# Sums of the hidden activations formed in the first feed-forward product, and one ring of buffers for results and pairs

## The chip, the core and the metric

The kernel runs on one core of one Trainium2 chip. The metric is device time in microseconds for one execution. Its engines are named here as in the profile: PE is TensorE (PEld its weight loads), ACT ScalarE, DVE VectorE, POOL GpSimd, SP SyncE. Each takes its instructions in the order of its own queue.

## The reference, cut to what matters

One decoder layer over 512 positions of width 2048. After a mixing half (attention, gating, convolution), the feed-forward half is

```python
h = rms_norm(x, mlp_norm[l])
x = x + jnp.square(jax.nn.relu(h @ w_mlp_in[l])) @ w_mlp_out[l]
```

with `w_mlp_in` 2048 x 8192 and `w_mlp_out` 8192 x 2048, all float32. The change touches these two products alone.

## The kernel before, in words

**Three matmuls for a product.** Each float32 operand is split into a high part (a rounding copy on ACT, `high` or `split`) and a low part (a subtraction on DVE, `low` or `split`); high x high, high x low and low x high are added in PSUM (`mm3`, lines 161 to 163). Activations are held transposed, 128 features by 512 positions a tile; `xh` and `xl` hold 16 such tiles.

**Groups.** `stream` runs a list of groups. A plain group (`tr_group`) makes 4 (or 2) output tiles over 16 steps k, loading 512 KB of weights for every two k ("a piece"); after each k, `step()` runs one task from a queue. A `Strassen` group ("a block", two output tiles) makes its 256 x 512 result with seven products instead of eight, in an order of two-by-two block sums: weights are added and subtracted on DVE (`s1`, `s2`, `q`), and the activations' sums lie ready in `tt`. A "double" product uses one 512-column matmul for high x both parts and one of 256 columns (lines 867, 868), and one DVE add more to join the halves; a "triple" uses three of 256 columns.

**The two feed-forward products.** The first: a plain group of 4 tiles, 29 blocks (products 0, 1 and 3 double), a plain group of 2 tiles. Each result gets its scale, the relu and the square (`hidden`: DVE, then ACT) and is stored to `hd` in DRAM by POOL. The second runs in four chunks of 2048 hidden features: chunk 0 has a plain group, 4 blocks and a closing plain group; chunks 1 to 3 have 6 blocks and a closing group. Results of chunks 0 to 2 are added to `x1d` in DRAM by storing DMAs that accumulate (`finish_out`, line 1018, and `close_mlp_out`, which first copies PSUM to tile `co` on ACT, line 1042); chunk 3 adds `x1d` on DVE and writes the output.

**Preparing a chunk.** While a closing group of chunks 0 to 2 runs, tasks (`both_tasks`) load the next chunk's hidden tiles in pairs (tile `hr`), write `xh`, `xl`, and form the sums from the pair in place (`sums`, four subtractions of 256 columns, line 936 on) for `tt`. For chunk 0 `parts_tasks` does this in two passes over the pairs, during the last group of the first product and the first of the second.

**Buffers.** Ring `hp` has three places of two tiles (4 KB a partition) for the pairs. The results `c` of a block and `co` of a closing group share one place, tag `c`.

**Order.** `ordr` pins an instruction behind the one traced before it on its engine, where `ordered[0]` is true: from `open_last_in`, so in the whole second product. Before that (`evac_qk` sets it false) the compiler's scheduler orders instructions; loads on POOL are never pinned. In `stream`, the load of an item (with its casts and subtractions) is traced two items ahead (`AHEAD`), so casts of weights stand in ACT's queue ahead of, or behind, tasks and result copies.

Of the kernel before, what the change touches and what calls it, by code (L numbers as in the profile page):

```python
# [9 lines left out]
F32 = mybir.dt.float32  # L10
F32R = mybir.dt.float32r
AF = mybir.ActivationFunctionType
ALU = mybir.AluOpType
AX = mybir.AxisListType

P = 128
T = 512
TB = T // P
D = 2048
KT = D // P  # L20
DFF = 4 * D
# [5 lines left out]
KC = CHUNK_FF // P  # L27
# [13 lines left out]
def trunk_kernel(  # L41
# [12 lines left out]
    nc = tc.nc  # L54
# [5 lines left out]
    w1 = w1[0].rearrange("(k p) n -> p k n", p=P)  # L60
    w2 = w2[0].rearrange("(k p) n -> p k n", p=P)

    dram = ctx.enter_context(tc.tile_pool(name="dram", bufs=1, space=bass.MemoryType.DRAM))
# [19 lines left out]
    def uid():  # L83
        cnt[0] += 1
        return cnt[0]
# [5 lines left out]
    def ordr(ins):  # L91
        return tc.keep_in_program_order(ins) if ordered[0] else ins
# [7 lines left out]
    def flush():  # L100
        while tasks:
            step()
# [24 lines left out]
    xh, xl = xhl[:, 0], xhl[:, 1]  # L127
# [4 lines left out]
    rbc = cpool.tile([P, T], F32, name="rbc")  # L132
# [595 lines left out]
    mlp = {}  # L728
# [8 lines left out]

    x1d = [dram.tile([P, T], F32, name=f"x1d{n}") for n in range(KT)]
    hd = [dram.tile([P, T], F32, name=f"hd{n}") for n in range(DFF // P)]
    nch = DFF // CHUNK_FF  # L740

    def open_out(ng):
# [38 lines left out]
    TH = T // 2  # L781

    def sub(out, a, b):
        ordr(nc.vector.tensor_tensor(out=out, in0=a, in1=b, op=ALU.subtract))  # L784

    def add(out, a, b):
        ordr(nc.vector.tensor_tensor(out=out, in0=a, in1=b, op=ALU.add))
# [23 lines left out]
    def x1mov(k):  # L811
        return x1v[:, k, :, 0], x1v[:, k, :, 1]

    class Strassen:


# [37 lines left out]
        def product(self, j, h, l):  # L854
            sp, i = mlp["spool"], self.i
            if j == 0 and self.begin is not None:
                self.begin(self)
            if j == 2:
                flush()
            if j < 6:  # L860
                self.pv = main_ps(f"pt{j}{i}").rearrange("p (h t) -> p h t", h=2)
            pv, half, double = self.pv, int(j == 6), j in self.double
            for m in range(KT // 2):
                start, stop = m == 0, m == KT // 2 - 1
                bh, bl, both = self.factor(FACTOR[j], m)
                if double:
                    nc.tensor.matmul(pv, lhsT=h[:, m], rhs=both, start=start, stop=False)  # L867
                    last[0] = nc.tensor.matmul(pv[:, 1], lhsT=l[:, m], rhs=bh, start=False, stop=stop)  # L868
                else:
                    mm3(pv[:, half], (h[:, m], l[:, m]), (bh, bl), start, stop)  # L870

            def take(out, more):
                add(out, pv[:, half], more)
                if double:
                    add(out, pv[:, 1], out)

            if j == 0:

                self.c = sp.tile([P, 6, TH], F32, tag="c", name=f"c{i}")
                self.p = [sp.tile([P, TH], F32, tag=f"p{n}", name=f"p{n}{i}") for n in range(2)]  # L880
            c = self.c
            if j in (0, 3):
                p = self.p[j // 3]
                ordr(nc.scalar.copy(out=p, in_=pv[:, 0]))
                if double:
                    add(p, pv[:, 1], p)
            elif j == 1:
                take(c[:, 2], self.p[0])
            elif j == 2:
                take(c[:, 0], self.p[0])  # L890
            elif j == 4:
                take(c[:, 1], c[:, 0])
                add(c[:, 0:6:5], self.p[1].unsqueeze(1).broadcast_to([P, 2, TH]), c[:, 0:2])
            elif j == 6:
                add(c[:, 3:5], pv, c[:, 0:2])
                self.finish(self, c[:, 2:6].rearrange("p (f h) t -> p f (h t)", f=2))

    def open_quarters():
        flush()
# [3 lines left out]
    def hidden(c, src, rb):  # L903

        ordr(nc.vector.scalar_tensor_tensor(out=c, in0=src, scalar=0.0, in1=rb, op0=ALU.max, op1=ALU.mult))
        ordr(nc.scalar.activation(out=c, in_=c, func=AF.Square))

    def finish_in(g, c):
        hidden(c, c, rbc.unsqueeze(1).broadcast_to([P, 2, T]))
        for n in range(2):  # L910
            nc.gpsimd.dma_start(out=hd[g.c0 // P + n], in_=c[:, n])

    def c_tiles(pss, name):
        for j, ps in enumerate(pss):
            if j % 2 == 0:
                cc = mlp["spool"].tile([P, 6, TH], F32, tag="c", name=f"{name}{j}").rearrange("p (f h) t -> p f (h t)", h=2)
            yield j, ps, cc[:, j % 2]

    def close_mlp_in(pss, f0):
        for j, ps, c in c_tiles(pss, f"cn{f0}"):  # L920
            hidden(c, ps, rbc)
            nc.gpsimd.dma_start(out=hd[f0 + j], in_=c)


    def pair(name):
        return mlp["spool"].tile([P, 2, T], F32, tag="hp", name=f"{name}{uid()}", bufs=3)

    def load_pair(c, m):
        t = pair("hr")
        for n in range(2):  # L930
            nc.gpsimd.dma_start(out=t[:, n], in_=hd[c * KC + 2 * m + n])
        return t

    def sums(t):
        q = t.rearrange("p k (h t) -> p (k h) t", h=2)
        sub(q[:, 0], q[:, 1], q[:, 0])
        sub(q[:, 1], q[:, 3], q[:, 1])
        sub(q[:, 3], q[:, 3], q[:, 0])
        sub(q[:, 2], q[:, 2], q[:, 3])
        return q  # L940

    def high(dst, src):
        ordr(nc.scalar.copy(out=dst, in_=src))  # L943

    def low(dst, src, h):
        sub(dst, src, h.bitcast(F32))

    def parts_tasks(c):

        room = [load_pair(c, m) for m in range(3)]  # L950
        s = [slice(2 * m, 2 * m + 2) for m in range(8)]

        def parts(m):
            if m < 8:
                high(xh[:, s[m]], room[m])
            if m:
                low(xl[:, s[m - 1]], room[m - 1], xh[:, s[m - 1]])
                room.append(load_pair(c, (m + 2) % 8) if m < 9 else None)

        def rest(m):  # L960
            t = room[8 + m]
            q = sums(t)
            high(mlp["tt"][:, :, m, 0], q)
            return q

        kept = {}

        def even(m):
            kept[m] = rest(m)

        def odd(m):
            low(mlp["tt"][:, :, m, 1], kept[m], mlp["tt"][:, :, m, 0])
            if m + 3 < 8:
                room.append(load_pair(c, m + 3))

        out = [lambda m=m: parts(m) for m in range(9)]
        for m in range(8):
            out.extend([lambda m=m: even(m), lambda m=m: odd(m)])
        return out

    def both_tasks(c):

        room = {m: load_pair(c, m) for m in range(3)}
        kept = {}

        def tile_high(k):
            if k < KC:
                high(xh[:, k], room[k // 2][:, k % 2])

        def tile_low(k):  # L990
            if 0 <= k < KC:
                low(xl[:, k], room[k // 2][:, k % 2], xh[:, k])

        def even(m):
            tile_high(2 * m)
            tile_low(2 * m - 1)
            if m:
                kept[m - 1] = sums(room[m - 1])
                high(mlp["tt"][:, :, m - 1, 0], kept[m - 1])

        def odd(m):
            tile_high(2 * m + 1)
            tile_low(2 * m)
            if m:
                low(mlp["tt"][:, :, m - 1, 1], kept[m - 1], mlp["tt"][:, :, m - 1, 0])
                if m + 2 < KC // 2:
                    room[m + 2] = load_pair(c, m + 2)

        return [f for m in range(KC // 2 + 1) for f in (lambda m=m: even(m), lambda m=m: odd(m))]

    def open_last_in():
        ordered[0] = True
# [26 lines left out]

    def close_mlp_out(pss, c, f0):  # L1040
        for j, ps, t in c_tiles(pss, f"co{c}{f0}"):
            ordr(nc.scalar.copy(out=t, in_=ps))
            nc.gpsimd.dma_start(out=x1d[f0 + j], in_=t, accum_op=ALU.add)

    def close_last(pss, f0, j, ts):
        dst = mlp["acc"][j // 2][:, j % 2, ts]
# [3 lines left out]
    def hmov(k):  # L1050
        return xh[:, k], xl[:, k]

    groups = [
        qk_group(0, 0, x_chunk), qk_group(1, 0), qk_group(0, 1), qk_group(1, 1),
        nat_group(w_in[:, :, OFF_V:OFF_V + 256], 256, xstat, close_v1),
        nat_group(w_in[:, :, OFF_V + 256:OFF_V + 768], 512, xstat4, close_v23),
        nat_group(w_in[:, :, OFF_VA:OFF_VA + 512], 512, xstat, close_va),
        nat_group(w_in[:, :, OFF_U:OFF_U + 512], 512, xstat, close_u),
    ]
# [7 lines left out]
        ))  # L1067
    groups.append(tr_group(w1[:, :, :T], 4, x1mov, lambda pss: close_mlp_in(pss, 0)))
    for c0 in range(T, DFF - 2 * P, 2 * P):
        groups.append(Strassen(w1, c0, x1_factor, (0, 1, 3), finish_in))  # L1070
    groups.append(tr_group(
        w1[:, :, DFF - 2 * P:], 2, x1mov, lambda pss: close_mlp_in(pss, DFF // P - 2), before=open_last_in,
    ))
# [62 lines left out]
```

## Time and profile before

| | |
|---|---|
| median of 3 runs | 2100.81 us (2098.47 to 2101.3) |
| the profiled execution's own time | 2099.07 us |
| its span, first to last instruction | 2097.4 us |
| mean granted clock of TensorE | 0.987 |
| busy, share of the span | PE 97%, PEld 88%, DVE 67%, ACT 39%, POOL 8% |
| first feed-forward product | from about 740 to 1360 us |
| second | from there to the end |

A row of a timeline gives the start, the duration, the engine, the line, what is written and read, and in brackets how long the engine was idle before and what ended it. A duration spans an instruction's whole way through its engine; consecutive matmuls overlap, so their pace is read from start to start. A row of windows gives the busy time of each engine in a stretch, with the instructions' count; PEclk is the granted clock as a share of full speed, and the DMA share is the mean busy share of the 16 DMA engines.

### The profile page before, as it was taken

Reading aid. Unit: us, or ns where it says so; the run is one execution under the profiler, and the core shown is the slowest. Engines: PE = TensorE matmul, PEld = TensorE weight load, DVE = VectorE, ACT = ScalarE, POOL = GpSimd, SP = SyncE. Lnnn points to the kernel's source line nnn. Section 1 sums busy time; section 2 is a strip of 40 time slices with the busy share of each in tenths; the row PEclk is TensorE's granted clock in tenths of the full one; section 3 lists DMA queues with packets and bytes.
Section 4 is the critical chain, followed back from the end, with each engine's and each line's share of the span. In section 5 each row is a group of like instructions: output and inputs, shape, how many; then the busy total and the mean of one; then the engine's idle time right before and its main releaser. Section 6 shows DMA issues by size and latency. Waiting matters only on the chain.

```text
span 2097.4 us, 30649 instructions
## 1 busy us (share of the span) xinstructions
PE 2034.8 (97%) x12434; PEld 1836.2 (88%) x12434; DVE 1395.6 (67%) x1846; ACT 820.6 (39%) x1086; POOL 158.0 (8%) x270
## 2 busy tenths in 40 slices
PE   9999999999999999999999999998979997997999
PEld 9999888888888889999999999877869986986998
DVE  5443453534345588888888888577678776777882
ACT  5334442322234434444444444443343443343441
POOL 0000000100000010000000000121010011001110
PEclk9999999999999999999999999999989998998999
DMA  7323222433533355444444444566545555554542
GB/s 250 124 76 105 79 67 70 129 99 97 185 129 126 116 152 155 127 130 138 125 140 128 130 144 122 159 194 136 156 129 142 121 171 125 133 154 121 161 142 90
DMA packets 322045, 276.78 MB, mean 132 GB/s; under 512 B 12772, under 2 KB 271076, under 8 KB 321904
## 3 DMA queue, kind: packets, MB, share of 16 engines
q1 hardware_dynamic: 295744, 202.93, 33.0%
q0 software_dynamic: 23712, 67.67, 11.7%
q10 hardware_dynamic: 2448, 4.23, 0.6%
q8 instruction: 97, 1.59, 0.3%
q14 instruction: 44, 0.36, 0.1%
HBM read 237.01 MB, written 37.77 MB: 131 GB/s over the span
## 4 chain that ended last, share of the span: by engine, by line
PE 77%; DMA 8%; DVE 8%; ACT 4%; issue 2%; POOL 0%; SPq 0%; ACTq 0%; DVEq 0%
PE pt L161 16%; PE pt L163 16%; PE pt L162 16%; PE pt L867 10%; PE pn L161 5%; PE pt L868 5%; PE pn L162 5%; PE pn L163 5%; DMA x1d<-c 4%; DVE wl L262 3%; DVE hr L784 2%; DMA wq<-in_w_mlp_out_dram 2%; ACT wh L261 2%; DMA x1d<-co 1%; ACT tt L943 1%
## 5 line engine op out<-in xcount | busy, mean ns | idle before, releaser
L163 PE MATMUL pt<-xhl,wl 128*128 128x256 f32 (+1 forms) x1480 | 493.5, 333 | 3.3 <-DVE wl L262 3.3
L161 PE MATMUL pt<-xhl,wh 128*128 128x256 f32 (+1 forms) x1480 | 493.7, 334 | 1.5 <-ACT xhl L943 1.5
L162 PE MATMUL pt<-xhl,wh 128*128 128x256 f32 (+1 forms) x1480 | 493.4, 333 | 1.1 <-DVE xhl L784 1.1
L262 DVE TENSOR_TENSOR wl<-wr,wh 128x1024 fp32r<-128x1024 f32 (+2 forms) x199 | 213.8, 1074 | 343.9 <-ACT wh L261 287.9
L261 ACT CAST wh<-wq 128x1024 fp32r<-128x1024 f32 x255 | 267.7, 1050 | 378.5 <-PE pt L162 190.7
L262 DVE TENSOR_TENSOR wl<-wq,wh 128x1024 fp32r<-128x1024 f32 x255 | 311.3, 1221 | 82.0 <-ACT wh L261 81.1
L261 ACT CAST wh<-wr 128x1024 fp32r<-128x1024 f32 (+2 forms) x199 | 185.0, 930 | 399.0 <-PE pt L162 265.0
L163 PEld LDWEIGHTS pt<-xhl,wl 128*128 128x128 f32 x1480 | 281.7, 190 | 31.7 <-DVE wl L262 4.5
L162 PEld LDWEIGHTS pt<-xhl,wh 128*128 128x128 f32 x1480 | 281.7, 190 | 28.9 <-DVE xhl L784 1.8
L161 PEld LDWEIGHTS pt<-xhl,wh 128*128 128x128 f32 x1480 | 281.3, 190 | 29.3 <-ACT xhl L943 2.1
L163 PE MATMUL pt<-tt,wl 128*128 128x256 f32 x1048 | 297.6, 284 | 3.8 <-DVE wl L262 3.6
L161 PE MATMUL pt<-tt,wh 128*128 128x256 f32 x1048 | 296.9, 283 | 1.8 <-ACT wh L261 1.8
L162 PE MATMUL pt<-tt,wh 128*128 128x256 f32 x1048 | 296.7, 283 | 0.0
L867 PE MATMUL pt<-tt,wh 128*128 128x512 f32 x584 | 215.1, 408 | 42.4 <-ACT wh L261 42.4
L161 PEld LDWEIGHTS pt<-tt,wh 128*128 128x128 f32 x1048 | 199.8, 191 | 6.4 <-ACT wh L261 3.0
L163 PEld LDWEIGHTS pt<-tt,wl 128*128 128x128 f32 x1048 | 199.9, 191 | 5.8 <-DVE wl L262 5.5
L162 PEld LDWEIGHTS pt<-tt,wh 128*128 128x128 f32 x1048 | 199.9, 191 | 0.0
L161 PE MATMUL pn<-wh,xhl 128*128 128x384 f32 (+2 forms) x512 | 185.2, 364 | 1.4 <-DVE qn L440 1.3
L162 PE MATMUL pn<-wl,xhl 128*128 128x384 f32 (+2 forms) x512 | 179.5, 351 | 0.7 <-DVE wl L148 0.7
L163 PE MATMUL pn<-wh,xhl 128*128 128x384 f32 (+2 forms) x512 | 179.2, 350 | 0.0
L867 PEld LDWEIGHTS pt<-tt,wh 128*128 128x128 f32 x584 | 112.7, 194 | 68.3 <-ACT wh L261 44.0
L868 PE MATMUL pt<-tt,wl 128*128 128x256 f32 x584 | 166.8, 287 | 1.9 <-DVE wl L262 1.9
(208 smaller groups left out, 2992.0 us busy)
## 6 DMA issues: line engine op xcount, KB each, us to landing
wq<-in_w_mlp_in_dram SPq DMA_DIRECT2D x116, 512.0 KB, 4.1
wq<-in_w_mlp_out_dram SPq DMA_DIRECT2D x88, 512.0 KB, 5.4
hr<-hd POOLq DMA_DIRECT2D x80, 256.0 KB, 3.1
wr<-in_w_mlp_out_dram SPq DMA_DIRECT2D x40, 512.0 KB, 4.5
wr<-in_w_in_dram SPq DMA_DIRECT2D x144, 128.0 KB, 2.3
wr<-in_w_out_dram SPq DMA_DIRECT2D x32, 512.0 KB, 3.6
hd<-c POOLq DMA_DIRECT2D x58, 256.0 KB, 2.6
wr<-in_w_in_dram SPq DMA_DIRECT2D x24, 512.0 KB, 3.5
```

The lines of the kernel that those rows point to most:

```text
L161: nc.tensor.matmul(ps, lhsT=ah, rhs=bh, start=start, stop=False)
L162: nc.tensor.matmul(ps, lhsT=ah, rhs=bl, start=False, stop=False)
L163: last[0] = nc.tensor.matmul(ps, lhsT=al, rhs=bh, start=False, stop=stop)
L261: ordr(nc.scalar.copy(out=dst_h, in_=src))
L262: ordr(nc.vector.tensor_tensor(out=dst_l, in0=src, in1=dst_h.bitcast(F32), op=ALU.subtract))
L784: ordr(nc.vector.tensor_tensor(out=out, in0=a, in1=b, op=ALU.subtract))
L867: nc.tensor.matmul(pv, lhsT=h[:, m], rhs=both, start=start, stop=False)
L868: last[0] = nc.tensor.matmul(pv[:, 1], lhsT=l[:, m], rhs=bh, start=False, stop=stop)
L943: ordr(nc.scalar.copy(out=dst, in_=src))
```

## The change

Results `c`, `co` and the pairs share one ring `hp`, now of four places. In the first product each pair of hidden tiles is also turned into its four sums, in another place of that ring, and stored to a new DRAM tensor `hs` by one DMA of 512 KB. The second product loads these sums where it formed them: `both_tasks` has eight steps of two tasks, each step with a pair and its sums, two steps loaded ahead; `parts_tasks` loads the sums in its second pass. In the first product, product 0 alone stays double. The three result columns of `c` that were spare are gone, its indices move. The last group of the first product, and the sums of the last pair, take places of the weights' ring `wq`.

```diff
+    hs = [dram.tile([P, 4, T // 2], F32, name=f"hs{n}") for n in range(DFF // P // 2)]
...
+    def pair(name):
+        return mlp["spool"].tile([P, 2, T], F32, tag="hp", name=f"{name}{uid()}", bufs=4)
...
-                self.c = sp.tile([P, 6, TH], F32, tag="c", name=f"c{i}")
+                self.c = pair("c").rearrange("p f (h t) -> p (f h) t", h=2)
...
-                add(c[:, 0:6:5], self.p[1].unsqueeze(1).broadcast_to([P, 2, TH]), c[:, 0:2])
+                take(c[:, 2], c[:, 1])
+                add(c[:, 1:4:2], self.p[1].unsqueeze(1).broadcast_to([P, 2, TH]), c[:, 1:3])
...
+    def store_hidden(f, c):
+        for n in range(2):
+            nc.gpsimd.dma_start(out=hd[f + n], in_=c[:, n])
+        t = pair("ts") if f + 2 < DFF // P else quarter_room("ts")
+        q, o = (v.rearrange("p k (h t) -> p (k h) t", h=2) for v in (c, t))
+        sub(o[:, 0:2], q[:, 1:4:2], q[:, 0:2])
+        sub(o[:, 3], q[:, 3], o[:, 0])
+        sub(o[:, 2], q[:, 2], o[:, 3])
+        nc.gpsimd.dma_start(out=hs[f // 2], in_=o)
+
     def finish_in(g, c):
         hidden(c, c, rbc.unsqueeze(1).broadcast_to([P, 2, T]))
-        for n in range(2):
-            nc.gpsimd.dma_start(out=hd[g.c0 // P + n], in_=c[:, n])
-
-    def c_tiles(pss, name):
+        store_hidden(g.c0 // P, c)
+
+    def c_tiles(pss, name, room=None):
+        room = room or pair
         for j, ps in enumerate(pss):
             if j % 2 == 0:
-                cc = mlp["spool"].tile([P, 6, TH], F32, tag="c", name=f"{name}{j}").rearrange("p (f h) t -> p f (h t)", h=2)
-            yield j, ps, cc[:, j % 2]
+                cc = room(f"{name}{j}")
+            yield j, ps, cc
...
-    def sums(t):
...
+    def load_sums(c, m):
+        t = pair("hsr").rearrange("p k (h t) -> p (k h) t", h=2)
+        nc.gpsimd.dma_start(out=t, in_=hs[c * KC // 2 + m])
+        return t
...
+        def sums(m):
+            if m < 8:
+                high(mlp["tt"][:, :, m, 0], room[8 + m])
+            if m:
+                low(mlp["tt"][:, :, m - 1, 1], room[7 + m], mlp["tt"][:, :, m - 1, 0])
+                if m + 3 < 8:
+                    room.append(load_sums(c, m + 3))
+
+        return [lambda m=m: parts(m) for m in range(9)] + [lambda m=m: sums(m) for m in range(9)]
+
+    def both_tasks(c):
+
+        room = {}
+
+        def load(m):
+            room[m] = load_pair(c, m), load_sums(c, m)
 
         def even(m):
-            kept[m] = rest(m)
+            high(xh[:, 2 * m], room[m][0][:, 0])
+            high(mlp["tt"][:, :, m, 0], room[m][1])
 
         def odd(m):
...
+            high(xh[:, 2 * m + 1], room[m][0][:, 1])
+            low(mlp["tt"][:, :, m, 1], room[m][1], mlp["tt"][:, :, m, 0])
+            s = slice(2 * m, 2 * m + 2)
+            low(xl[:, s], room[m][0], xh[:, s])
+            if m + 2 < KC // 2:
+                load(m + 2)
+
+        load(0)
+        load(1)
+        return [f for m in range(KC // 2) for f in (lambda m=m: even(m), lambda m=m: odd(m))]
...
-        groups.append(Strassen(w1, c0, x1_factor, (0, 1, 3), finish_in))
+        groups.append(Strassen(w1, c0, x1_factor, (0,), finish_in))
```

## Rows read from the trace of the kernel before

**Rows 1.** Windows of 100 us; the sum is over all four such stretches.
```profile
core 0: us, PE busy (x) PEld busy (x) DVE busy (x) ACT busy (x) POOL busy (x), PEclk, DMA share, GB/s
1700.00:1800.00 100.00, 85.79 (x526) 76.32 (x525) 74.92 (x100) 40.91 (x52) 14.67 (x22) 0.93 0.52 132
...
sum 400.00, PE 345.31 PEld 311.82 DVE 300.55 ACT 159.24 POOL 59.11; mean PE 86.33 PEld 77.96 DVE 75.14 ACT 39.81 POOL 14.78
```

**Rows 2.** Waits, whole span: engine, line, waited for: us, times, longest.
```profile
DVE c L787 <- DMA x1d<-c: 50.1, 13, 4.6
...
PE pt L867 <- ACT wh L261: 42.4, 5, 11.3
...
ACT co L1042 <- DMA x1d<-co: 32.8, 4, 8.7
```

**Rows 3.** Timeline of ACT, POOL and PE at the third chunk boundary.
```profile
1735.40 0.61 ACT L943 CAST xhl<-hr 128x512 fp32r<-128x512 f32 x1
1735.92 1.06 ACT L1042 COPY co<-pt 128x512 f32<-128x512 f32 x2
1736.80 1.77 POOL L1043 DMA_DIRECT2D x1d<-co  x2 [5.61 <-ACT co L1042]
1745.61 1.07 ACT L1042 COPY co<-pt 128x512 f32<-128x512 f32 x2 [8.63 <-DMA x1d<-co]
1746.57 1.06 ACT L261 CAST wh<-ws 128x1024 fp32r<-128x1024 f32 x1
1747.68 0.79 PE L867 MATMUL pt<-tt,wh 128*128 128x512 f32 x1 [11.23 <-ACT wh L261]
```

**Rows 4.** Window of that boundary, columns as in the first group.
```profile
1730.00:1760.00 30.00, 16.25 (x95) 13.57 (x94) 18.48 (x26) 10.59 (x16) 6.89 (x10) 0.77 0.47 103
```

**Rows 5.** Timeline of DVE in chunk 1's closing group, from piece to piece.
```profile
1704.75 1.23 DVE L262 TENSOR_TENSOR wl<-wr,wh 128x1024 fp32r<-128x1024 f32 x1 [0.24 <-ACT wh L261]
1706.49 1.80 DVE L784 TENSOR_TENSOR hr<-hr 128x256 f32<-128x256 f32 x4
...
1710.88 1.23 DVE L262 TENSOR_TENSOR wl<-wr,wh 128x1024 fp32r<-128x1024 f32 x1 [0.25 <-ACT wh L261]
```

**Rows 6.** Windows: chunk 1's closing group; chunk 0's first group and preparation.
```profile
1690.00:1728.00 38.00, 38.00 (x169) 31.48 (x168) 31.32 (x48) 17.98 (x24) 5.39 (x10) 1.00 0.55 163
1350.00:1400.00 50.00, 49.84 (x220) 40.97 (x219) 34.20 (x44) 22.98 (x26) 13.87 (x26) 1.00 0.75 242
```

**Rows 7.** Timeline of PE, one first-product block: first matmul of products 0, 2, 3, 4, 5.
```profile
938.84 0.40 PE L867 MATMUL pt<-xhl,wh 128*128 128x512 f32 x1
...
944.49 0.28 PE L161 MATMUL pt<-tt,wh 128*128 128x256 f32 x1
...
947.38 0.40 PE L867 MATMUL pt<-tt,wh 128*128 128x512 f32 x1
...
950.19 0.28 PE L161 MATMUL pt<-tt,wh 128*128 128x256 f32 x1
...
953.07 0.28 PE L161 MATMUL pt<-xhl,wh 128*128 128x256 f32 x1
```

**Rows 8.** Window of that block.
```profile
938.84:958.83 19.99, 19.99 (x147) 18.88 (x145) 17.38 (x21) 8.83 (x10) 1.07 (x2) 1.00 0.44 132
```

**Rows 9.** Groups by line and form, whole span: count, busy us, mean ns, idle before.
```profile
L787 DVE TENSOR_TENSOR c<-p,c 128x512 f32<-128x512 f32 x51 | 35.3, 692 | 1.7
...
L787 DVE TENSOR_TENSOR p<-pt,p 128x256 f32<-128x256 f32 x80 | 33.5, 418 | 5.0 <-ACT p L884 5.0
```

**Rows 10.** Timeline of POOL in chunk 2's first block: two loads issued.
```profile
1756.51 1.13 POOL L931 DMA_DIRECT2D hr<-hd  x2 [7.23 <-issue]
```

**Rows 11.** DMA issues, 1350 to 1400 us: count, size, median us to landing.
```profile
hr<-hd POOLq DMA_DIRECT2D x24, 256.0 KB, 4.3
wr<-in_w_mlp_out_dram SPq DMA_DIRECT2D x7, 512.0 KB, 5.8
```

**Rows 12.** DMA issues, whole span, the same weights.
```profile
wr<-in_w_mlp_out_dram SPq DMA_DIRECT2D x40, 512.0 KB, 4.5
```

**Rows 13.** Groups by line, 960 to 1300 us, DVE: 17 blocks of the first product.
```profile
L262 DVE TENSOR_TENSOR wl<-wq,wh 128x1024 fp32r<-128x1024 f32 x85 | 103.9, 1222 | 35.1 <-ACT wh L261 35.1
```

More of the change, by code (lines that the diff above doesn't have):

```diff
@@ L887, in product @@
             elif j == 1:
-                take(c[:, 2], self.p[0])
+                take(c[:, 0], self.p[0])
             elif j == 2:
-                take(c[:, 0], self.p[0])
+                take(c[:, 1], self.p[0])
             elif j == 4:
-                take(c[:, 1], c[:, 0])
-                add(c[:, 0:6:5], self.p[1].unsqueeze(1).broadcast_to([P, 2, TH]), c[:, 0:2])
+                take(c[:, 2], c[:, 1])
+                add(c[:, 1:4:2], self.p[1].unsqueeze(1).broadcast_to([P, 2, TH]), c[:, 1:3])
             elif j == 6:
-                add(c[:, 3:5], pv, c[:, 0:2])
-                self.finish(self, c[:, 2:6].rearrange("p (f h) t -> p f (h t)", f=2))
+                add(c[:, 1:3], pv, c[:, 1:3])
+                self.finish(self, c.rearrange("p (f h) t -> p f (h t)", f=2))
     def open_quarters():
@@ L906, in hidden, with quarter_room @@
         ordr(nc.scalar.activation(out=c, in_=c, func=AF.Square))
+    def store_hidden(f, c):
[7 more added lines that the diff above has]
+        nc.gpsimd.dma_start(out=hs[f // 2], in_=o)
     def finish_in(g, c):
         hidden(c, c, rbc.unsqueeze(1).broadcast_to([P, 2, T]))
-        for n in range(2):
-            nc.gpsimd.dma_start(out=hd[g.c0 // P + n], in_=c[:, n])
-    def c_tiles(pss, name):
+        store_hidden(g.c0 // P, c)
+    def c_tiles(pss, name, room=None):
+        room = room or pair
         for j, ps in enumerate(pss):
             if j % 2 == 0:
-                cc = mlp["spool"].tile([P, 6, TH], F32, tag="c", name=f"{name}{j}").rearrange("p (f h) t -> p f (h t)", h=2)
-            yield j, ps, cc[:, j % 2]
+                cc = room(f"{name}{j}")
+            yield j, ps, cc
+    def quarter_room(name):
+        return mlp["spool"].tile([P, KT // 2, P], F32, tag="wq", name=name, bufs=3).rearrange("p k n -> p (k n)").rearrange("p (f t) -> p f t", f=2)
     def close_mlp_in(pss, f0):
[L920 to L926, printed above, removed]
+        for j, ps, c in c_tiles(pss, f"cn{f0}", quarter_room if f0 else None):
+            hidden(c[:, j % 2], ps, rbc)
+            if j % 2:
+                store_hidden(f0 + j - 1, c)
     def load_pair(c, m):
@@ L932, in load_pair @@
         return t
-    def sums(t):
[L935 to L940, printed above, removed]
+    def load_sums(c, m):
+        t = pair("hsr").rearrange("p k (h t) -> p (k h) t", h=2)
+        nc.gpsimd.dma_start(out=t, in_=hs[c * KC // 2 + m])
+        return t
     def high(dst, src):
@@ L948, in parts_tasks @@
     def parts_tasks(c):
-        room = [load_pair(c, m) for m in range(3)]
+        room = [load_pair(c, m) for m in range(4)]
         s = [slice(2 * m, 2 * m + 2) for m in range(8)]
@@ L957, in parts @@
                 low(xl[:, s[m - 1]], room[m - 1], xh[:, s[m - 1]])
[L958 to L966, printed above, removed]
+                room.append(load_pair(c, m + 3) if m < 5 else load_sums(c, m - 5))
+        def sums(m):
[5 more added lines that the diff above has]
+                    room.append(load_sums(c, m + 3))
@@ L968, in even @@
+        return [lambda m=m: parts(m) for m in range(9)] + [lambda m=m: sums(m) for m in range(9)]
[3 more added lines that the diff above has]
+            room[m] = load_pair(c, m), load_sums(c, m)
         def even(m):
-            kept[m] = rest(m)
+            high(xh[:, 2 * m], room[m][0][:, 0])
+            high(mlp["tt"][:, :, m, 0], room[m][1])
         def odd(m):
-            low(mlp["tt"][:, :, m, 1], kept[m], mlp["tt"][:, :, m, 0])
-            if m + 3 < 8:
-                room.append(load_pair(c, m + 3))
@@ L976, in parts_tasks @@
[L976 to L1009, printed above, removed]
+            high(xh[:, 2 * m + 1], room[m][0][:, 1])
@@ L1041, in close_mlp_out @@
         for j, ps, t in c_tiles(pss, f"co{c}{f0}"):
-            ordr(nc.scalar.copy(out=t, in_=ps))
-            nc.gpsimd.dma_start(out=x1d[f0 + j], in_=t, accum_op=ALU.add)
+            ordr(nc.scalar.copy(out=t[:, j % 2], in_=ps))
+            nc.gpsimd.dma_start(out=x1d[f0 + j], in_=t[:, j % 2], accum_op=ALU.add)
     def close_last(pss, f0, j, ts):
```

## The prediction, made before the changed kernel ran

> **What bounds the kernel now.** I read the windows first. TensorE is busy without a break through the whole first product and most of the second; in four stretches of 100 us it is not, and they read alike: about 86 us busy, a granted clock of 0.93. Together they hold 400 - 345.3 = 54.7 us of idle TensorE [rows 1]. The view of waits says where: 42.4 us of it are five waits of the product at L867 for a weight cast on ScalarE, the longest 11.3 us, and beside them stand two waits for stores into x1d, 32.8 us of ScalarE (tile co) and 50.1 us of VectorE (tile c) [rows 2]. The timeline of the third chunk boundary ties these together. ScalarE copies two result tiles of the closing group, which fill the only "c" buffer; their adding stores go out at 1736.80; the next two copies start at 1745.61, 8.63 us idle, when those have landed; the cast of the next block's weights stands behind them in the queue, and TensorE resumes at 1747.68 after 11.23 us [rows 3]. The clock row of that boundary is 0.77 of full over 30 us, so 0.23 x 2 x 30 = 13.8 us at 1.2 instead of 2.4 GHz [rows 4]. There are four such places, one after each closing group of chunks 0 to 2 and one after the first group of chunk 0. A second cause lies ahead of each: VectorE, which forms the sums, needs 1710.88 - 1704.75 = 6.13 us a piece of two k [rows 5]. TensorE needs 38 / 169 = 0.225 us a matmul [rows 6], 24 of them 5.4 us. After eight pieces VectorE is 8 x 0.73 = 5.8 us behind.
>
> **The change, part by part.**
>
> *Results in a ring of four.* The second pair of co copies takes another buffer, so the 8.63 us wait goes [rows 3], and with it the long gap; the blocks' c no longer waits for its own last store (50.1 us on VectorE [rows 2], most of it off TensorE's path). What is late next at a boundary is the cast behind four copies: 2 x 1.06 + 1.06 us on ScalarE and 1.23 us on VectorE after the group's end, 4.4 us, against the two products of 2.88 us that TensorE has in hand [rows 3, 5, 7]. It fits with 1.3 us to spare.
>
> *Sums loaded instead of formed, in the second product.* Four subtractions of 1.80 us in all go from each piece [rows 5]. VectorE is left with three of 1.23 us (weights, sums, one of 1024 columns in place of two of 512), 3.7 us against 5.4; ScalarE has 1.06 + 1.06 + 2 x 0.61 = 3.3 us [rows 3]. Both keep up, so the smaller gaps of the boundaries go too. I credit the whole 54.7 us.
>
> *The clock.* Of 13.8 us at the low level, 11.23 may lie inside the gap [rows 3, 4]; then 2.6 us of work ran at half speed and lost 1.3 us, 5 us over four boundaries. Had all 13.8 been work, it would be 6.9 each, 28 in all. The first matmul after the gap still takes 0.79 us where others take 0.40 [rows 3, 7], so the gap holds most of it: I take 8.
>
> *One double product in the first product.* A triple of three 256-column matmuls takes 953.07 - 950.19 = 2.88 us; the double on the sums 950.19 - 947.38 = 2.81; two doubles together 944.49 - 938.84 = 5.65, 2.825 each [rows 7]. Two become triples: 0.07 + 0.055 = 0.125 us a block, 29 blocks, +3.6 us. Nothing hides it, since TensorE has no idle time there [rows 8].
>
> *Sums formed and stored there.* VectorE loses two adds of 0.42 us and gains one subtraction of 512 columns at 0.69 and two of 256 at 0.42 to 0.45 [rows 5, 9]: 17.38 - 0.84 + 1.57 = 18.1 of 20.1 us a block [rows 8]. The first one waits for ScalarE's Square of c (1.06 us by the same shape [rows 3]), and the weight splits behind it wait along. The order there is the compiler's. Bounds: 0, if they fall into idle time; a gain is excluded, as TensorE is full; above, see the third rival. I take 0. POOL issues one store of 512 KB more a block, and the stream rises from 132 by 0.52 MB / 20 us to 158 GB/s [rows 8].
>
> *The chunk-0 preparation* loads sums where it loaded pairs again: equal bytes, no subtractions, one issue instead of two. The first and last groups of the first product form sums once each, beside TensorE's work; nothing.
>
> *New waits in the three closing groups.* Here is the cost I can least see. Each step now loads a pair (two issues) and its sums (one), and only two steps fit the ring, where three pairs did. The fourth buffer is the last block's c, free when its adding store has landed, some 9 us by the one seen [rows 3]; until then POOL's queue stands, with the second step's sums and the loads behind. They come about 0.6 + 5.8 us later, some 16 us into the group, where the third k wants them at 3 x 2.7 + 0.7 = 9. Behind that wait on ScalarE stand the weight casts, two pieces (10.8 us) ahead, so this first delay costs nothing. But each later load set is issued after its own buffers are read and must land within 10.8 us less the work of a step (about 5 us): 5.8 us, against three issues of 0.57 [rows 10] and a landing of 4.3 (256 KB) to 5.8 us (512 KB) where traffic was 242 GB/s [rows 6, 11], 6.0 to 7.5. So part of the delay lasts to the group's end. Price: from nothing (landings shorter than shown) up to the old boundary in full, 13.75 us of idle TensorE [rows 4], three times: 0 to 41 us. VectorE's lag of 5.8 us today explains only the small part, 13.75 - 11.23 = 2.5 us, of that idle. A lag of that order is what I expect, so I take 2 us each, 6 in all.
>
> The Trainium skill (DMA: Bandwidth & Descriptors, Anatomy of one DMA) prices a transfer on POOL's path at about 2.0 us plus bytes at 436 GB/s, which would put the 512 KB of sums at an estimated 3.2 us, every set in time, and the sum at 2040. The trace speaks against it under load: by that rule 256 KB take 2.6 us, and the row says 4.3 [rows 11].
>
> *Sum*, against the profiled execution (2099.07 us, 0.08% under the median of 2100.81): 2099.07 - 54.7 - 8 + 3.6 + 6 = **2046 us**, -2.6%. A measurement of this kernel tells about 0.2% (4 us) from no change.
>
> **Rivals.**
>
> *The loads come late (2070).* A closing group carried 163 GB/s; seven loads of sums (3.7 MB in 38 us) make that 260, above the 242 at which the DMA engines' share was 0.75 [rows 6]. If landings then grow so that the loop of two steps sets the pace, each group runs 6 us longer and the clock falls again: 3 x 8 = 24 us. Against it: in that stretch of 242 GB/s TensorE lost 0.16 us in 50. The skill's same page (Issuing engines are not separate DMA queues) says that queues of all issuers end on the same 16 engines; by that rule the weights suffer with the sums, and the trace agrees: weights of 512 KB took 5.8 us there, 4.5 over the whole run [rows 11, 12].
>
> *The ring does not free the results (2083).* A load of pairs for the next chunk goes out at 1756.51, a whole chunk ahead of its use [rows 10]. If such early loads may take ring places, they hold three of four while the blocks run, and results have one again: 8 us at each of four boundaries and some 5 us of clock and block waits come back, 37 us. For it speaks that the loads run so early; against it, that buffers of one ring should be given out in the program's order.
>
> *VectorE becomes the bound of the first product (2115, slower).* VectorE works 18.1 us of 20.1, and in 17 blocks it already idled 35.1 us before the weight splits, 2.1 a block [rows 13]. If that stays and the new subtractions wait 2.3 us on Square (its own 1.06 and a cast ahead of it), the block is 18.1 + 2.1 + 2.3 = 22.5 us: 2.4 us of stall 29 times, +70. The point from which it decides: waits of over 2.0 us a block. Against it: the 2.1 us are mostly slack before early splits, which shrink when VectorE is late.
>
> **How the numbers follow.** Forecast 0.65 (alone 2028 to 2060), late loads 0.18, ring not freed 0.09, VectorE 0.08. The range 2028 to 2078: below, no new wait (-6) and 20 instead of 8 us of clock; above, the first rival whole and part of the second. Left out are the third and the dearer half of the second. Faster 0.90 (the first three, less mixtures); within 0.2% 0.03, where a mild third eats the gain; slower 0.07.
>
> **What would show it.** Right: no gap over 3 us at L867, no wait of co or c for x1d, clock 1.0 nearly throughout from 1400 us on, blocks of the first product of 20.1 us. Wrong: VectorE or ScalarE waiting long for a load of sums in the closing groups, POOL standing behind a store, gaps before weight splits in the first product, or an unchanged wait of co.

## The result, and the profile after

The changed kernel takes 2046.65 us (median of 4 runs, 2045.39 to 2047.94) beside 2100.22 us of the kernel before on the same chip: ratio 0.9746 [0.9729, 0.9763], 2.5% faster. Its profiled execution took 2046.41 us, with a span of 2044.6 us (before 2097.4) and a mean granted clock of 0.997 (before 0.987). The predicted time was 2046 us. Of all executions reported here one, of the kernel with the doubles back, took 5125.37 us where its four others took 2036.53 to 2041.33; it is left out.

Where the time went is read from two windows, one from the first block's first product on the sums to the last block's last in the first product (29 blocks), one from there to the last matmul. First the kernel before, then the changed one:

```profile
core 0: us, PE busy (x) PEld busy (x) DVE busy (x) ACT busy (x) POOL busy (x), PEclk, DMA share, GB/s
764.60:1338.50 573.90, 573.90 (x4146) 542.39 (x4145) 494.69 (x574) 253.04 (x288) 33.64 (x63) 1.00 0.45 135
1338.50:2093.80 755.30, 699.49 (x4449) 633.78 (x4449) 541.95 (x672) 292.33 (x351) 99.35 (x154) 0.96 0.54 144
```

```profile
765.00:1342.80 577.80, 577.44 (x4601) 566.74 (x4600) 508.31 (x603) 252.66 (x288) 46.49 (x87) 1.00 0.52 156
1342.80:2041.00 698.20, 687.15 (x4450) 629.48 (x4450) 499.69 (x526) 293.81 (x351) 111.58 (x178) 0.99 0.63 179
```

The first product takes 3.9 us more, the second 57.1 us less. In the second, TensorE's idle time falls from 755.3 - 699.5 = 55.8 to 11.05 us. Its busy time falls too, by 12.3 us, though it does the same work. Part of that is the clock: at the low level the same matmul takes longer (of 256 columns, 0.21 us from start to start behind the gap shown below, 0.12 ahead of it). The rest is split in the section on the prediction. The stretch that answers to [rows 1], and the block of the first product that answers to [rows 8]:

```profile
1700.00:1800.00 100.00, 94.61 (x688) 90.40 (x688) 82.02 (x89) 41.35 (x50) 10.52 (x13) 0.97 0.58 136
...
958.83:978.93 20.10, 20.10 (x162) 19.72 (x162) 17.79 (x21) 8.82 (x11) 1.61 (x3) 1.00 0.53 157
```

The waits of the changed kernel's second product (engine, line, waited for: us, times, longest) answer to [rows 2]. Neither ScalarE (co) nor VectorE (c) waits for x1d any more, and the product's wait for a cast, 42.4 us, is gone. In their place:

```profile
ACT tt L955 <- DMA hsr<-hs: 63.1, 24, 7.1
POOL hr L946 <- DVE tt L785: 60.5, 15, 8.5
...
POOL hsr L951 <- DMA x1d<-c: 20.8, 3, 7.8
...
PE pt L162 <- DVE xhl L785: 9.4, 3, 3.9
```

The timeline of chunk 1's closing group (picked from POOL, ACT, DVE and PE, in order of time) shows how these four belong together:

```profile
1657.36 1.77 POOL L1012 DMA_DIRECT2D x1d<-c  x2 [10.27 <-DVE c L788]
...
1665.28 0.56 POOL L951 DMA_DIRECT2D hsr<-hs  x1 [6.15 <-DMA x1d<-c]
...
1671.12 1.05 ACT L955 CAST tt<-hsr 128x1024 fp32r<-128x1024 f32 x1 [5.94 <-DMA hsr<-hs]
...
1695.82 1.05 ACT L955 CAST tt<-hsr 128x1024 fp32r<-128x1024 f32 x1 [7.10 <-DMA hsr<-hs]
...
1707.12 1.22 DVE L785 TENSOR_TENSOR xhl<-hr,xhl 128x1024 fp32r<-128x1024 f32 x1
...
1708.39 0.58 PE L162 MATMUL pt<-xhl,wh 128*128 128x256 f32 x1 [3.92 <-DVE xhl L785]
```

POOL issues the adding store of the last block's c, then stands 6.15 us until it has landed, since the second step's sums need that ring place. The sums arrive at 1671; ScalarE, with the weight casts behind it, has stood 5.94 us. The lag is never made up: each later load waits for its own place, the step for 1695.82 comes 7.10 us late, and at 1708.39 the last step's low part is 3.92 us late for TensorE. The result copies (co x4, at 1705.75, 2.04 us) now follow without a break. In the traffic of 1656 to 1706 us the listing of DMA issues shows what the loads met there (count, size, median us to landing):

```profile
hsr<-hs POOLq DMA_DIRECT2D x7, 512.0 KB, 6.8
hr<-hd POOLq DMA_DIRECT2D x12, 256.0 KB, 4.7
wr<-in_w_mlp_out_dram SPq DMA_DIRECT2D x4, 512.0 KB, 5.4
wq<-in_w_mlp_out_dram SPq DMA_DIRECT2D x3, 512.0 KB, 8.5
```

The Trainium skill (DMA: Bandwidth & Descriptors, Anatomy of one DMA) would give 512 KB an estimated 3.2 us. In the first product, at 156 GB/s, the stores of sums (hs<-ts, 30 of them) took 3.4 us, which agrees; here, at 221 GB/s, the same bytes took 6.8.

### The profile page after: what moved, and what is told of

Read it like the earlier page. It is cut to its first block, busy times and chain, and to the rows that moved or that the text cites. A ratio compares the mean times of both kernels' runs of the same rounds, so it can differ in the third digit from the quotient of the medians.

```text
span 2044.6 us, 31582 instructions
## 1 busy us (share of the span) xinstructions
PE 2026.2 (99%) x12898; PEld 1856.6 (91%) x12898; DVE 1367.0 (67%) x1732; ACT 822.3 (40%) x1086; POOL 183.1 (9%) x318
## 4 chain that ended last, share of the span: by engine, by line
PE 90%; DMA 5%; DVE 3%; issue 1%; ACT 1%; POOL 0%; SPq 0%; DVEq 0%; POOLq 0%; ACTq 0%
PE pt L163 21%; PE pt L162 21%; PE pt L161 21%; PE pt L871 7%; PE pn L161 5%; PE pn L162 5%; PE pn L163 5%; PE pt L872 3%; DMA hsr<-hs 2%; DMA hr<-hd 1%; DMA x1d<-c 1%; DVE xhl L785 1%; DVE wl L262 1%; DVE tt L785 1%; PE sc L529 0%
## 5 line engine op out<-in xcount | busy, mean ns | idle before, releaser
L162 PE MATMUL pt<-xhl,wh 128*128 128x256 f32 (+1 forms) x1712 | 560.0, 327 | 9.4 <-DVE xhl L785 9.4
L163 PE MATMUL pt<-xhl,wl 128*128 128x256 f32 (+1 forms) x1712 | 559.7, 327 | 1.7 <-DVE wl L262 1.7
L161 PE MATMUL pt<-xhl,wh 128*128 128x256 f32 (+1 forms) x1712 | 560.5, 327 | 0.0
L163 PE MATMUL pt<-tt,wl 128*128 128x256 f32 x1280 | 362.3, 283 | 0.4 <-DVE wl L262 0.4
L162 PE MATMUL pt<-tt,wh 128*128 128x256 f32 x1280 | 362.3, 283 | 0.0
L161 PE MATMUL pt<-tt,wh 128*128 128x256 f32 x1280 | 362.2, 283 | 0.0
L162 PEld LDWEIGHTS pt<-xhl,wh 128*128 128x128 f32 x1712 | 326.7, 191 | 37.1 <-DVE xhl L785 10.2
L163 PEld LDWEIGHTS pt<-xhl,wl 128*128 128x128 f32 x1712 | 326.6, 191 | 29.6 <-DVE wl L262 2.5
L161 PEld LDWEIGHTS pt<-xhl,wh 128*128 128x128 f32 x1712 | 326.5, 191 | 28.4 <-issue 0.2
L163 PEld LDWEIGHTS pt<-tt,wl 128*128 128x128 f32 x1280 | 245.1, 191 | 0.6 <-DVE wl L262 0.6
L261 ACT CAST wh<-ws 128x1024 fp32r<-128x1024 f32 x102 | 107.3, 1052 | 132.6 <-PE pt L162 56.6
L262 DVE TENSOR_TENSOR wl<-ws,wh 128x1024 fp32r<-128x1024 f32 x102 | 124.3, 1218 | 5.1 <-ACT wh L261 3.3
L871 PE MATMUL pt<-tt,wh 128*128 128x512 f32 x352 | 125.3, 399 | 0.0
```

Of the source, the lines that this page charges most:

```text
L161: nc.tensor.matmul(ps, lhsT=ah, rhs=bh, start=start, stop=False)
L162: nc.tensor.matmul(ps, lhsT=ah, rhs=bl, start=False, stop=False)
L163: last[0] = nc.tensor.matmul(ps, lhsT=al, rhs=bh, start=False, stop=stop)
L261: ordr(nc.scalar.copy(out=dst_h, in_=src))
L262: ordr(nc.vector.tensor_tensor(out=dst_l, in0=src, in1=dst_h.bitcast(F32), op=ALU.subtract))
```

## The experiments

Ten kernels ran on three occasions beside the kernel before, whose median was 2098.9 to 2101.9 us. What is compared with the changed kernel is taken by the ratio to before, or by windows.

**The yardstick.** The changed kernel, unaltered.

> The changed kernel again, unaltered, as the yardstick for the three kernels that run beside it on this chip. Every theory: 2046 to 2047 us, 0.9745 of the kernel before; a chip may shift both by some tenths of a per cent, so the others are compared with this run.

Measured: 2045.29 us (2038.09 to 2047.23), 0.9729 [0.9711, 0.9746]. Its second product took 695.3 us with 8.9 idle, in the profiled run before it 698.2 with 11.05. The remaining waits vary from run to run by several us, so differences of 2 to 3 us are read from windows, not from times.

**One part alone: only the ring.** Edit of the kernel before (c takes the layout of four halves of the change; sums and doubles as before):

```
-        ... name=f"{name}{uid()}", bufs=3)
+        ... name=f"{name}{uid()}", bufs=4)
...
-                self.c = sp.tile([P, 6, TH], F32, tag="c", name=f"c{i}")
+                self.c = pair("c").rearrange("p f (h t) -> p (f h) t", h=2)
...
-                cc = mlp["spool"].tile([P, 6, TH], F32, tag="c", ...
+                cc = pair(f"{name}{j}")
```

> The kernel before with one part of the change alone: results c and co go into one ring of four with the loaded pairs (before: one buffer of their own, and three for pairs). Sums are still formed in the second product and the three double products stay. Theory (the split of the prediction: of 13.75 us idle at a boundary 11.23 are the wait for the stores, the rest VectorE's lag): the co and c waits for x1d go at all four boundaries, gaps of 2 to 3 us stay at those where sums are formed; 2100 - 45 - 5 of clock = about 2050 (2045 to 2056). Rival: VectorE's lag of about 6 us was covered by the wait for the stores and takes its place; gaps of 6 to 9 us stay at the closing groups, 2065 to 2085.

Measured: 2058.93 us, 0.981 [0.9795, 0.9825]. This lies between the two ranges, nearer to the theory's. Its second product in the windows, and the third boundary in the timeline (DVE, ACT, PE):

```profile
1338.40:2053.20 714.80, 696.57 (x4451) 632.96 (x4449) 549.85 (x672) 292.03 (x351) 98.97 (x154) 0.98 0.56 152
```

```profile
1710.18 1.80 DVE L784 TENSOR_TENSOR hr<-hr 128x256 f32<-128x256 f32 x4
...
1713.48 2.04 ACT L1042 COPY co<-pt 128x512 f32<-128x512 f32 x4
...
1715.39 1.07 ACT L261 CAST wh<-ws 128x1024 fp32r<-128x1024 f32 x1
...
1716.52 0.79 PE L870 MATMUL pt<-tt,wh 128*128 128x512 f32 x1 [2.51 <-ACT wh L261]
```

The copies run without the 8.63 us break of [rows 3], and the gap is 2.51 us, as expected of VectorE's lag. With the small gaps beside it 18.2 us stay idle in all. What the theory missed is the clock: busy time is 696.6 us, only 2.9 under before. Windows across the gap and after it show why, first of the kernel before, then of this one:

```profile
1738.20:1747.68 9.48, 0.00 (x0) 0.00 (x0) 0.02 (x1) 2.07 (x4) 1.70 (x4) 0.50 0.71 166
1747.68:1751.80 4.12, 3.65 (x11) 2.85 (x12) 4.02 (x7) 0.79 (x2) 1.59 (x2) 0.50 0.75 99
```

```profile
1714.01:1716.52 2.51, 0.00 (x1) 0.01 (x1) 1.46 (x3) 2.51 (x6) 2.16 (x4) 0.70 0.34 39
1716.52:1721.80 5.28, 4.81 (x15) 3.82 (x16) 4.55 (x7) 1.95 (x3) 1.37 (x2) 0.50 0.87 165
```

The long gap spent 9.48 us of its low clock idle and left 4.12 us of work at 1.2 GHz; the short one was followed by 5.28 us of it. So it is over the whole second product: the time that TensorE worked at the low level is 20.32 us before, in five stretches, and 20.57 us here, in four. The first stretch before, 3.41 us, lies behind a gap of only 2.08 us.

```profile
1410.44:1413.85 3.41, 3.41 (x18) 3.41 (x18) 2.23 (x5) 2.02 (x3) 0.42 (x1) 0.50 0.10 41
...
sum 54.61, PE 20.32 PEld 16.64 DVE 19.35 ACT 16.34 POOL 10.68; mean PE 4.06 PEld 3.33 DVE 3.87 ACT 3.27 POOL 2.14
```

```profile
sum 23.89, PE 20.57 PEld 15.76 DVE 18.80 ACT 11.90 POOL 7.58; mean PE 5.14 PEld 3.94 DVE 4.70 ACT 2.98 POOL 1.89
```

Gaps cut to about a quarter kept their whole price in clock.

**One part undone: one place for co.** Edit of the changed kernel (with the two partial sums p kept in free places of c, for room):

```
+    def own(name):
+        return mlp["spool"].tile([P, 2, T], F32, tag="c", name=f"{name}{uid()}", bufs=1)
...
-                self.p = [sp.tile([P, TH], F32, tag=f"p{n}", name=f"p{n}{i}") for n in range(2)]
+                self.p = [self.c[:, 2], self.c[:, 3]]
...
-        for j, ps, t in c_tiles(pss, f"co{c}{f0}"):
+        for j, ps, t in c_tiles(pss, f"co{c}{f0}", own):
```

> The changed kernel with one part undone: the two pairs of result tiles (co) of each closing group share one buffer of their own again; the blocks' c stays in the ring of four, which no longer holds co; sums are stored and loaded as changed (the room comes from the two partial sums p, kept in free places of c). Theory: the second pair of copies waits some 8 us for the stores of the first, ScalarE's queue stands, the casts of the next block's weights behind it: a gap of 7 to 10 us at each of the four boundaries, with some 1 to 2 us of half clock each: 2046 + 4 x 10 = 2080 to 2088. Rival: the lag of forming the sums was what made those gaps long, so with sums loaded the wait has slack: gaps under 4 us, 2048 to 2062.

Measured: 2063.51 us, 0.9835 [0.9819, 0.9851]. The wait came back, most of its price did not. Timeline of the second boundary (ACT, PE), and the second product's window:

```profile
1547.68 1.07 ACT L1039 COPY co<-pt 128x512 f32<-128x512 f32 x2 [6.32 <-DMA x1d<-co]
...
1548.56 1.72 POOL L1040 DMA_DIRECT2D x1d<-co  x2 [5.61 <-ACT co L1039]
...
1548.64 1.06 ACT L261 CAST wh<-ws 128x1024 fp32r<-128x1024 f32 x1
...
1549.75 0.56 PE L874 MATMUL pt<-tt,wh 128*128 128x512 f32 x1 [3.85 <-ACT wh L261]
```

```profile
1343.20:2058.30 715.10, 694.66 (x4450) 634.00 (x4449) 499.32 (x526) 293.36 (x351) 111.46 (x178) 0.98 0.62 175
```

ScalarE waits 6.32 us, TensorE 3.85: without VectorE's lag about 2.5 us of the wait are covered, and the gaps stay under 4 us, which is the rival's mechanism. (At the third boundary the changed kernel's own wait, 3.91 us here, is still there beside it.) It lies 1.5 us beyond the rival's time. So the two parts overlap: in the second product the ring alone saves 755.3 - 714.8 = 40.5 us, the sums with one place for co 40.2, both together 57.1. In this kernel the blocks' c stays in the ring; no kernel ran that loads the sums with c and co both in one place as before.

**Five places in the ring.** Edit of the changed kernel: p in c as above, and

```
-        ... tag="hp", name=f"{name}{uid()}", bufs=4)
+        ... tag="hp", name=f"{name}{uid()}", bufs=5)
```

> The changed kernel with five places in the ring in place of four (the room comes from the two partial sums p, kept in the places of c that are still free). Theory: in the closing groups of chunks 0 to 2 POOL stands up to 7.8 us behind the adding store of the last block's c, because that c holds the fourth place; this delay makes the three TensorE waits of 2.9, 3.9 and 2.5 us and most of the half-clock stretch behind them. With a fifth place both steps' loads go out at once, so about 9 to 11 us of idle and 3 to 4 of clock go: 2032 to 2036. Rival: the loop is set by landings (median 7.1 us for a load of sums at 230 GB/s), not by the place: POOL's wait behind the store goes, the waits for loads of sums stay as long, 2043 to 2047.

Measured: 2030.79 us (2030.01 to 2031.26), 0.9665 [0.9652, 0.9679]. This is the theory's side, slightly below its range. Windows: the second product, and chunk 1's closing group.

```profile
1342.40:2025.50 683.10, 682.48 (x4450) 624.98 (x4449) 499.92 (x526) 294.82 (x351) 111.53 (x178) 1.00 0.64 183
```

```profile
1650.00:1698.00 48.00, 48.00 (x231) 40.49 (x230) 31.65 (x28) 26.78 (x35) 11.39 (x20) 1.00 0.76 240
```

682.5 us at clock 1.00 is what this work takes; idle time and the busy time above it are the loss: before 55.8 + 17.0, ring alone 18.2 + 14.1, one place for co 20.4 + 12.2, changed 11.05 + 4.7 us. Landings are no shorter here (over the whole run sums 7.6 us, pairs 7.5, where the changed kernel has 7.1 and 5.6), and the traffic of the closing group is 240 GB/s. POOL still stands three times behind an adding store (14.8 us in all, in the view of waits), but it is the store of the block ahead of the last, and the second step's sums go out before the closing group begins:

```profile
1644.03 0.54 POOL L951 DMA_DIRECT2D hsr<-hs  x1 [5.29 <-DMA x1d<-c]
```

The loads were not too slow; one set was asked for too late. The new home of p is not what helped: the kernel with one place for co keeps p in c as well, and there the wait in chunk 1's closing group stayed (3.91 us), as did ScalarE's waits for sums (61.0 us, 23 times).

**Is it that one c?** Four places as changed, but the c of the block ahead of each closing group has a buffer of its own:

```
-                self.c = pair("c")...
+                self.c = (own if self.src is not w1 and self.c0 == KT * P - T - 2 * P else pair)("c")...
```

> The changed kernel, four places in the ring as changed, but the c of the one block ahead of each closing group has a buffer of its own (the room again from keeping the partial sums p in free places of c). Theory: what the changed kernel still loses (11 us idle in four places and 4.7 us of clock) comes from that one c, which holds the fourth place while the second step's sums ask for it; so this kernel is as fast as the one with five places: 2030 to 2034. Rival: the fifth place helped because the loads could run a step further ahead at all times; then this kernel gains little: 2038 to 2046.

Measured: 2030.83 us (2030.65 to 2035.36), 0.9671 [0.9657, 0.9685], the same as five places. The timeline of POOL has no wait behind that c's store (issued at 1658.47). As with five places, the wait now comes a block earlier, where nothing needs the sums yet (19.8 us in three waits over the run):

```profile
1646.51 0.56 POOL L954 DMA_DIRECT2D hsr<-hs  x1 [6.30 <-DMA x1d<-c]
1658.47 1.72 POOL L1015 DMA_DIRECT2D x1d<-c  x2 [11.40 <-DVE c L788]
1663.36 1.13 POOL L949 DMA_DIRECT2D hr<-hd  x2 [3.17 <-DVE tt L785]
1665.13 0.54 POOL L954 DMA_DIRECT2D hsr<-hs  x1 [0.63 <-DVE xhl L785]
```

The profiled execution was its slowest (2035.36 us); the 3.5 us for which TensorE idled there lie elsewhere, 2.4 of them in chunk 0's first group. That c, holding the place that the second step's sums ask for, is the cause.

**The doubles back.** Edit of the changed kernel:

```
-        groups.append(Strassen(w1, c0, x1_factor, (0,), finish_in))
+        groups.append(Strassen(w1, c0, x1_factor, (0, 1, 3), finish_in))
```

> The changed kernel with the three double products (0, 1, 3) back in the first product; all else as changed. Theory (the term +3.6 us of the sum): two triples become doubles again, 0.125 us a block, 29 blocks, so 3.6 us less than the changed kernel: about 2043. VectorE gets two adds of 0.42 us a block back, 17.8 + 0.8 = 18.6 of 20.0 us, which still fits. Rival (VectorE is the bound in waiting): the two adds push it over, TensorE gets gaps in the first product, and the time is 2047 or more. Second rival: the difference of the two shapes, read off one block, is no real one: 2046 to 2047.

Measured: 2036.53 to 2041.33 us, 0.9705 [0.9691, 0.9718] against the yardstick's 0.9729, which is 0.0024 x 2100 = 5 us less. The intervals overlap, so the times alone do not show it. The first product's window says how much of that is the edit:

```profile
764.70:1338.50 573.80, 573.80 (x4145) 542.28 (x4144) 526.34 (x660) 252.09 (x286) 46.02 (x86) 1.00 0.52 156
```

573.8 against 577.8: 4.0 us, no gap on TensorE, with VectorE at 526 of 574. The rest is taken for the variation of the waits in the second product.

**No subtractions in the first product.** Edit of the changed kernel, which leaves the sums out of the computation:

```
-        t = pair("ts") if f + 2 < DFF // P else quarter_room("ts")
...
-        nc.gpsimd.dma_start(out=hs[f // 2], in_=o)
+        nc.gpsimd.dma_start(out=hs[f // 2], in_=c.rearrange("p k (h t) -> p (k h) t", h=2))
```

> The changed kernel without the three subtractions a pair in the first product: the activations themselves are stored where the sums were, so the second product's sums are left out of the computation; stores, loads and TensorE's work are the same. Theory (the sums were costed at 0 there): 2046 to 2047, as the changed kernel, with VectorE's share of a block of the first product down by 1.57 us from 17.8. Rival (the wait for Square and the three subtractions cost something in each block or after the ring's use by the sums): faster than the changed kernel by over 3 us, 2043 or less.

Measured: 2044.01 us, 0.973 [0.9715, 0.9745], no different from the yardstick. The first product takes 577.2 us there, 577.8 with the subtractions; VectorE's busy time falls from 508.3 to 473.6 us. The sums cost TensorE 0.6 us by these windows (1.1 by the yardstick's 578.3), near the 0 of the prediction.

**Where VectorE would become the bound.** The subtractions done two and three times over (edit: `for _ in range(2):` or `range(3)` ahead of the three `sub` lines of `store_hidden`).

> The changed kernel with the three subtractions of a pair of the first product done twice over (the same values in the same places), 1.57 us more on VectorE a block: 17.8 + 1.6 = 19.4 of 20.1 us. It looks for the point at which VectorE would become the bound of the first product. Theory (its idle time ahead of the weight splits is slack that shrinks): TensorE does not notice, 2045 to 2048. Rival (the third rival of the prediction: 2.1 us of idle a block stay whatever the load): 19.4 + 2.1 - 20.1 = 1.4 us of stall, 29 times, 40 us: about 2085.

> The same with the three subtractions done three times, 3.1 us more on VectorE a block: 17.8 + 3.1 = 20.9 of 20.1 us, so VectorE cannot keep up in any order. Theory: a block takes VectorE's 20.9 us, 0.8 us more, 29 times, 24 us: 2066 to 2074, a little more where the clock falls. Rival (idle of 2.1 us stays on top): 20.9 + 2.1 - 20.1 = 2.9 us a block, 84 us: about 2130.

Measured: 2057.83 us (0.9797 [0.9781, 0.9813]) and 2059.19 us (0.9799 [0.9784, 0.9814]). Both expectations missed: twice is not free, and three times costs no more than twice. The first product takes 590.7 and 586.1 us, against 577.8. The blocks of the doubled kernel took 20.1 to 21.4 us, those of the tripled one mostly 20.11 with some of 21.3. Four blocks of the tripled kernel in a window, and its waits of VectorE in the first product:

```profile
1011.16:1092.26 81.10, 80.37 (x638) 78.63 (x638) 80.68 (x110) 35.88 (x41) 6.43 (x12) 1.00 0.51 158
```

```profile
DVE wl L262 <- ACT wh L261: 7.1, 6, 2.1
```

VectorE is busy 80.68 of 81.10 us and TensorE still loses only 0.7. In the changed kernel VectorE waited 45.2 us for these casts in the same stretch, so that idle time is slack that shrinks under load. What both traces do show is that casts wait for weights: from 765 to 1352 us ScalarE waited 104.1 us for their loads in the doubled kernel and 82.2 us in the tripled one, 4.4 us in the changed kernel. The doubled kernel's row:

```profile
ACT wh L261 <- DMA wq<-in_w_mlp_in_dram: 104.1, 26, 5.1
```

Why the weights come later, and why the doubled kernel loses more with more idle on VectorE (44.6 us), was not settled; the order of instructions there is the compiler's.

**Both gains.** Five places and the three doubles.

> Five places in the ring and the three double products of the kernel before. Theory: TensorE works without a break in both products (683 us in the second with five places), and the doubles take 3.9 us less in the first (573.9 against 577.8 us): 2030.8 - 3.9 = 2027 (2026 to 2028). Rival: the VectorE adds that the doubles bring back (526 us of 574 busy in the first product) cost TensorE time now that nothing else does: 2030 or more.

Measured: 2027.19 us (2025.55 to 2027.64), 0.9646 [0.9633, 0.966]: faster than both kernels, and within the range that adds its two parts. The second product is 682.3 us with 681.8 busy; TensorE's own work is all that is left there.

## Why the prediction was right

The total is right to 1 us. Its sign and its cause are right: all four signs that it named for this showed (no gap over 3 us ahead of a block, no wait of co or c for x1d, the clock near 1.0, blocks of 20.1 us). Two of its signs of being wrong showed as well: ScalarE waits long for sums in the closing groups, and POOL stands behind a store. The nearness of the total is in part luck: by the terms of the sum, two errors of about 9 us met with opposite signs.

- **The idle time credited, -54.7.** It was 55.8, all in the second product, and all of it went. That both parts of the change were needed for it, as the prediction argued from the wait for the stores and VectorE's lag, is shown by the two kernels that each leave one cause standing.
- **The clock, -8.** Too small. Busy time beyond the clean 682.5 us was 17.0 us before, so 17.0 stood to be won, and only part of it is the clock. TensorE worked 20.32 us at the low level; half of that, 10.2 us, is what full speed saves. The failing step is the placing of the 13.8 us of low clock mostly inside the gap: at the last three boundaries 4.74, 3.62 and 4.66 us of work ran at half speed, not 2.6, and at the first 7.31 us, part of it ahead of the long gap. The other 6.8 us the sum did not have at all. They are not clock but short stalls that the listing hides: a queued matmul of 256 columns starts 0.12 us after the one before but is listed at 0.28 us, so that 0.16 us of a stall behind it counts as busy. Summed over the traces outside the low stretches, what the starts lose against their usual pace beyond the listed idle is 6.6 us more before than with five places.
- **The doubles, +3.6.** 3.9 and 4.0 us by windows.
- **The sums in the first product, 0.** Right. VectorE's block is 17.79 us, not 18.1, since queued instructions overlap (below): without the three subtractions the first product has 34.7 us less of VectorE, 1.2 us a block and not the 1.57 of the sum. 157 GB/s was forecast as 158.
- **The new waits, +6.** The mechanism is as written: the place held by the last block's c, POOL's queue standing, a first delay that costs nothing, a lag kept to the group's end. Two steps of its price failed. 2 us a group was too little: 2.93, 1.47 + 3.92 and 2.53 us, 11 in all. And the clock behind new gaps was not counted: 9.39 us of work at the low level, 4.7 us. Together 15.7 in place of 6.

So -55.8 - 17.0 + 3.9 + 15.7 = -53.2, against -52.8 us of span.

Of the rivals, late loads had half of a truth. The loop of two steps does keep the lag, but landings are not what it hangs on: with that c out of the way the same traffic costs nothing. By the Trainium skill (DMA: Bandwidth & Descriptors, Issuing engines are not separate DMA queues) the transfers of all issuers run on the same 16 DMA engines, so weights should suffer with the sums; the trace agrees, with 8.5 us for wq in the closing group against 5.1 over the second product. The ring did free the results, as the missing wait of co shows. VectorE did not bind: its decision point was put at 2.0 us of waits a block on the ground that 2.1 us of idle might stay, and under three times the subtractions it did not stay.

## What to carry to other kernels

When a store holds a buffer of a ring that loads share, look at who asks for that place next: here one result tile ahead of each closing group, held for its store's landing, cost 15.7 us of 2046, and one more place, found by keeping partial sums in result places not yet written, took nearly all of it back. Two causes of one gap do not add: the ring alone won 40 us, the sums with one cause left standing 40, both 57. Price a gap with the clock behind it, and do not scale that part with the gap's length.

## What the runs showed of the hardware

- After idle gaps of 2.51 and 11.23 us TensorE's granted clock stood at 0.5, and 5.28 and 4.12 us of work followed at that level; the shorter gap left more of it. In the changed kernel 5.72 us of work followed its gap of 3.92 us so. Not every gap costs this: behind its gap of 2.93 us, which ends at 1538.39, the clock stayed at 1.00.
- VectorE's queued instructions of 1024 columns are listed at 1.22 us but start 1.13 to 1.14 us apart, so durations summed overstate a full queue by 7%. Three such starts of the tripled kernel:

```profile
1008.22 1.21 DVE L785 TENSOR_TENSOR wq<-wq,wq 128x1024 f32<-128x1024 f32 x1
1009.36 1.22 DVE L909 SCALAR_TENSOR_TENSOR c<-c,rbc 128x1024 f32<-128x1024 f32 x1
1010.49 1.22 DVE L262 TENSOR_TENSOR wl<-ws,wh 128x1024 fp32r<-128x1024 f32 x1
```
